# A hybrid attention block on one core: dense steps dealt out anew at the start of the attention, and GpSimd's low parts cut into four

## The chip, the core and the metric

The kernel runs on one core of one Trainium2 chip. TensorE multiplies matrices, VectorE and ScalarE work on tiles and read the products out of PSUM, GpSimd does a few elementwise operations and issues some of the DMAs, SyncE issues most of the others. The engines run side by side, each through its own instructions in a fixed order, and wait for each other by semaphores. The metric is the device time in microseconds (us) of one execution; less is better.

## The reference

One layer on 512 tokens of width 1024, in float32. `proj` is split into queries, keys and values of two attentions and into two gates; both attentions are gated, merged and followed by a feed-forward network and a gated embedding.

```python
proj = rms_norm(x, g_mix[i]) @ w_in[i]
(q_n, kc_n, vc_n, ks_n, vs_n, kw_n, vw_n, gate_n,
 q_m, k_m, v_m, gate_a, gate_b) = jnp.split(proj, IN_CUTS, axis=-1)
y_nsa = nsa_mixer(q_n, kc_n, vc_n, ks_n, vs_n, kw_n, vw_n, gate_n, pos_pad, ...)[:, :s]
y_moba = moba_mixer(q_m, k_m, v_m, pos_pad, ...)[:, :s]
merged = (jax.nn.sigmoid(gate_a[:, :s]) * (y_nsa @ w_up_nsa[i])
          + jax.nn.sigmoid(gate_b[:, :s]) * (y_moba @ w_up_moba[i]))
x = x + merged @ w_out[i]
gate, up = jnp.split(rms_norm(x, g_ffn[i]) @ w_ffn_in[i], 2, axis=-1)
x = x + (jax.nn.silu(gate) * up) @ w_ffn_out[i]
ple_gate = jax.nn.sigmoid(rms_norm(x, g_ple[i]) @ w_ple_gate[i])
x = x + ple_gate * (p[i] @ w_ple_proj[i])
```

With 512 tokens the attentions come down to causal softmax attention: 8 heads of MoBA with one set of keys, and 8 heads of NSA with two sets (selected and window) and 32 compressed keys besides.

## The kernel before

**Number format.** A float32 operand is split into a high part (`wh`, rounded to float32r by ScalarE, L128) and a low part (`wl`, the rest, by subtraction, L133 or L135). A product is three matmuls: high by high, high by low, low by high (`tmm`, L466 to L472). `Weights` keeps a list of weight units of 128x1024. SyncE's DMAs bring them into `wr` (three buffers); `get` splits units ahead of use (`depth` 2, in the attention 3) into `wh` and `wl` (four buffers each). Low parts are made by VectorE. Only for units of the kinds "ga" and "um", once `between` is set, GpSimd makes them (L131 to L133), in its order behind a one-column copy called "seen" (L977) of the last job's normalized probabilities. `between` is set for the first time after the attention's third step. GpSimd also issues the DMAs that add blocks of feed-forward weights in memory for a later stage (`add`, L278 and L281), each behind a "seen".

**The attention.** `attention(jobs)` (from L880) is a generator that yields after each step. It runs 24 jobs, 8 of MoBA and 16 of NSA; there are 192 steps. A job has four score tiles `sb`, for query tiles 3, 2, 0 and 1, of 512, 384, 128 and 256 columns; each is two matmuls (L893 with the key's high part, L894 with the low one). The tiles of 384 and 128 columns lie in one PSUM bank, and two banks take turns. VectorE masks a tile and finds its extreme (L896, into `p` and `am`), ScalarE takes the exponential (L898), and `normalize` (L903 to L913) scales by one over the sum, three tiles on VectorE and the one of 512 columns on ScalarE (L911). Then `turn` transposes the ten blocks of `p` (L921, tile `pt`), which are split into `pw` and `phl` (L930 ScalarE, L931 VectorE), and `apply` multiplies them by the values (L940 to L945, tile `pv`). `finish_head` (L867 to L876) adds the halves of a head's result and splits pairs of heads into YM or YN: `yt` on ScalarE, `yf` on VectorE, the high part on ScalarE, the low part on VectorE. `KN` (L548, L549) are keys of NSA that a side chain still turns meanwhile.

**The dense steps.** `fill` is a chain of the gate products (`gates`, tiles `ga`, 16 weight units) and MoBA's projection (`up`, tiles `umo`, 4 units). A step is one `tmm` of 3 x 512 columns; 8 steps make a unit, 160 the whole chain. Its purpose is work for TensorE that needs nothing of the softmax. The order in which steps are issued is written by hand at L1040 to L1045. `weave` deals out a share of a dense step per attention step: 0.95 for the first 80, 0.65 after (FILL_RATE, L35), and a quarter of a step of the side chain. Dense steps left over stand behind the attention. Behind all this comes NSA's projection (tiles `uno`), whose last quarter needs the last pair of heads.

**The order on the engines.** The framework puts the instructions of all engines into order by its own estimate of when each can run, starting from the order of issue; `issue_after` adds constraints, among them that a dense step stands behind the scores or transposes issued before it (`anchors`). So a moved step changes the order on TensorE, VectorE and ScalarE at other places, too.

Of the kernel before, what the change touches and what calls it, by code (L numbers as in the profile page):

```python
# [10 lines left out]
F32 = mybir.dt.float32  # L11
# [3 lines left out]
OP = mybir.AluOpType  # L15
# [16 lines left out]
WARM = 9  # L32
BIG_BUFS = 34
AHEAD = 7
FILL_RATE = (0.95, 0.65, 80)  # L35
BEFORE_UM = 3
BEGUN = 2
SCALE = "vvva"
# [23 lines left out]
class Weights:  # L62
# [42 lines left out]
    def parts(self):  # L105
        i = self.n_split
        self.load(i + 1)
        self.n_split += 1
        key, src, n, tag = self.units[i]
        if isinstance(src, str):  # L110
            t, q = (self.kept[x] for x in src.split("+"))
            with self.tc.issue_after(self.low):
                self.nc.vector.tensor_add(t[:, :n], t[:, :n], q[:, :n])
        else:
            t = self.raw.pop(i)
        if key[0] == "fo" and not isinstance(src, str):
            self.kept[key[3]] = t
        if isinstance(src, tuple) and None in src:
            k = 512 * src.index(None)
            with self.tc.issue_after(self.low):  # L120
                self.nc.vector.tensor_add(t[:, k:k + 512], self.last[:, :512], self.last[:, 512:])  # L121
        self.last = t
        h = self.pool.tile([128, 1024], F32R, name=f"wh{i}", tag="wh", bufs=4)
        l = self.pool.tile([128, 1024], F32R, name=f"wl{i}", tag="wl", bufs=4)
        self.done[i] = (h, l)
        for a, b in self.pieces(i, n):
            for c, d in self.halves(i, n) if i else [(a, b)]:
                self.begun = self.nc.scalar.activation(h[:, c:d], t[:, c:d], AF.Copy).ins  # L128
            if i == a == 0:
                yield  # L130
            if self.between is not None and key[0] in ("ga", "um"):  # L131
                with self.tc.issue_after(self.between):
                    self.low = self.nc.gpsimd.tensor_tensor(l[:, a:b], t[:, a:b], h[:, a:b].bitcast(F32), op=OP.subtract).ins  # L133
            else:
                self.low = self.nc.vector.tensor_sub(l[:, a:b], t[:, a:b], h[:, a:b].bitcast(F32)).ins  # L135
            yield
# [17 lines left out]
def run(gen):  # L154
    for _ in gen:
        pass


def weave(main, side, ratio=1.0, later=None, turn=0):

    acc, alive = 0.0, True
    for n, _ in enumerate(main):
        acc += ratio if later is None or n < turn else later
        while acc >= 1.0 and alive:
            acc -= 1.0
            try:
                next(side)
            except StopIteration:
                alive = False
        yield  # L170
    if alive:
        yield from side
# [8 lines left out]
def chain(*gens):  # L181
    for g in gens:
        yield from g
# [12 lines left out]
def steps(gen, n):  # L196
    for _ in range(n):
        next(gen, None)
# [18 lines left out]
def hybrid_kernel(ctx: ExitStack, tc: tile.TileContext, a, out):  # L217
# [333 lines left out]
    def turned(parts, tag, dst, gain):  # L551


        b = bank("tb", tag)
        for t, x in enumerate(parts):
            T.transpose(b[:, tts(t)], x, ident)
        for i in range(2):
            half = slice(64 * i, 64 * i + 64)
            last = split_turned((b[half], half), dst[:, i], gain)
        return last  # L560
# [118 lines left out]
    def gates(i0, i1, tag="a"):  # L679
        for i in range(i0, i1):  # L680
            o = bank("ga", tag)
            yield from ttile(("ga", i), o)
            z = GT[i]
            V.tensor_tensor(z, o, rb0, op=OP.mult)
            A.activation(z, z, AF.Tanh)
# [324 lines left out]
    def up(nm, Y, done):  # L1010
        for i in range(4):
            wh, wl = W.get((nm, i))
            os = []
            for j in range(2):
                o = bank(nm + "o", "a")
                os.append(o)
                for kt in range(4):
                    tmm(o, wh, wl, j * 4 + kt, Y[0][kt], Y[1][kt], kt == 0, kt == 3)
                    yield
                done(2 * i + j, o)  # L1020
# [9 lines left out]
    att = attention(jobs)  # L1030
# [9 lines left out]
    fill = chain(gates(8, 16), gates(0, BEFORE_UM), up("um", YM, up_moba_done), gates(BEFORE_UM, 8))  # L1040
    W.depth = 3
    steps(fill, 4)
    steps(att, 1)
    steps(fill, 4)
    run(weave(weave(att, fill, *FILL_RATE), side, 0.25))  # L1045

# [170 lines left out]
    class Blocks:  # L1217
# [14 lines left out]
        def split(self, j, *parts):  # L1232
            for src, names in parts:
                n = len(names) * CH
                nm = f"{self.name}{j}{names[0]}"
                if n == 1024:
                    h, l = flat(t4(nm + "h")), flat(t4(nm + "l"))
                elif n == 512:
                    r = t4(nm)
                    h, l = r[:, 0], r[:, 1]  # L1240
                else:
                    if j % 2 == 0:
                        self.third = t4(nm)
                    h, l = (self.third[:, j % 2, half(k)] for k in range(2))
                A.activation(h, src, AF.Copy)
                V.tensor_sub(l, src, h.bitcast(F32))  # L1246
                for k, x in enumerate(names):
                    self.at[j, x] = h[:, half(k)], l[:, half(k)]
# [278 lines left out]
```

## Time and profile before

| | |
|---|---|
| median of three runs | 815.98 us (815.6 to 816.95) |
| the profiled execution's own time | 815.51 us |
| its span, from the first to the last instruction | 813.8 us |
| attention with dense steps, from its first scores to its last product | 147.2 to 354.7 us of the span |
| GpSimd's 16 low parts | 160.2 to 324.0 us of the span, 2.39 to 2.69 us each |
| granted TensorE clock | 1.00 |

The profile is one execution. PE is TensorE's matmuls, PEld its weight loads, DVE VectorE, ACT ScalarE, POOL GpSimd. A timeline row has start, duration, engine, line, operation, output and inputs; in brackets stands the idle time of the engine ahead of it and what ended that. Ends of matmuls are modelled, so they overlap; the distance between starts tells the pace. Line numbers are those of the kernel before; in the changed kernel they are 2 higher from L133 on, and 4 higher from L1044 on.

### The profile page before, as it was taken

How to read it: one execution, taken by the hardware profiler on the slowest of the kernel's cores; microseconds unless marked ns; L12 is line 12 of the kernel's file. 1: busy time of each engine (PE TensorE's matmuls, PEld its weight loads, DVE VectorE, ACT ScalarE, POOL GpSimd, SP SyncE). 2: the span in 40 equal slices, each digit the busy share in tenths (PEclk: the TensorE clock that was granted, in tenths of full speed). 3: DMA queues.
4: the chain of work that ended last, by engine and by line, in shares of the span. 5: the costliest groups of instructions: out<-in, count | busy, mean ns of one | idle time of the engine just before them, and what ended most of it. 6: DMA issues, size and time to landing. Idle time of an engine off the chain costs nothing.

```text
span 813.8 us, 13180 instructions
## 1 busy us (share of the span) xinstructions
PE 807.0 (99%) x4821; PEld 717.5 (88%) x4821; DVE 628.0 (77%) x1165; ACT 490.0 (60%) x941; POOL 177.7 (22%) x210
## 2 busy tenths in 40 slices
PE   9999999999999999999999999999999999999997
PEld 7889898788888888888888999988999989998886
DVE  6889777887777867849467888887888887889744
ACT  6456555867777777734366666644666644665631
POOL 2826245333333413116010011000111000010000
PEclk9999999999999999999999999999999999999999
DMA  9434659598877758645424244444344343461612
GB/s 339 160 121 125 216 137 281 168 235 231 222 240 153 222 144 211 168 126 176 182 89 149 78 130 131 143 145 139 114 146 133 129 155 117 131 233 66 195 38 91
DMA packets 45361, 130.43 MB, mean 160 GB/s; under 512 B 5232, under 2 KB 5616, under 8 KB 41328
## 3 DMA queue, kind: packets, MB, share of 16 engines
q1 hardware_dynamic: 39376, 92.87, 34.9%
q0 software_dynamic: 4416, 32.51, 16.1%
q10 hardware_dynamic: 1504, 4.21, 1.6%
q8 instruction: 38, 0.62, 0.3%
q14 instruction: 27, 0.22, 0.1%
HBM read 122.22 MB, written 36.70 MB: 195 GB/s over the span
## 4 chain that ended last, share of the span: by engine, by line
PE 98%; DVE 1%; DMA 0%; ACT 0%; issue 0%; SPq 0%
PE sa L472 5%; PE sa L471 5%; PE sa L470 5%; PE ga L470 4%; PE ga L472 4%; PE ga L471 4%; PE nt L1115 3%; PE nt L1117 3%; PE nt L1116 3%; PE pt L921 3%; PE sv L1381 2%; PE sv L1384 2%; PE sv L1383 2%; PE sc L472 2%; PE sc L471 2%; PE sc L470 2%
## 5 line engine op out<-in xcount | busy, mean ns | idle before, releaser
L128 ACT ACTIVATE wh<-wr 128x512 fp32r<-128x512 f32 (+2 forms) x263 | 204.4, 800 | 179.9 <-PE sc L471 29.5
L135 DVE TENSOR_TENSOR wl<-wr,wh 128x1024 fp32r<-128x1024 f32 (+2 forms) x187 | 215.5, 1162 | 69.6 <-ACT wh L128 68.2
L896 DVE CUSTOM_DVE_ANT_0 p<-sb,big_mask 128x512 f32<-128x512 f32 (+1 forms) x96 | 45.6, 486 | 13.2 <-PE sb L894 12.5
L470 PE MATMUL ga<-xh,wh 128*128 128x512 f32 x128 | 53.0, 414 | 0.0
L472 PE MATMUL ga<-xh,wl 128*128 128x512 f32 x128 | 50.2, 393 | 0.0
L471 PE MATMUL ga<-xl,wh 128*128 128x512 f32 x128 | 50.1, 391 | 0.0
L1299 POOL TENSOR_TENSOR hg<-zg,u 128x256 f32<-128x256 f32 x10 | 10.4, 1038 | 156.7 <-ACT zg L1298 156.7
L1299 POOL TENSOR_TENSOR hf<-zg,u 128x256 f32<-128x256 f32 x10 | 15.9, 1588 | 128.3 <-DVE h L1246 110.9
L133 POOL TENSOR_TENSOR wl<-wr,wh 128x1024 fp32r<-128x1024 f32 x16 | 40.7, 2542 | 0.1
L931 DVE TENSOR_TENSOR pw<-pt,pw 128x512 fp32r<-128x512 f32 x48 | 32.5, 685 | 7.7 <-ACT pw L930 7.6
L921 PE MATMUL pt<-ident,p 128*128 128x128 f32 x240 | 36.6, 273 | 0.0
L921 PEld LDWEIGHTS pt<-ident,p 128*128 128x128 f32 x240 | 29.0, 140 | 4.7 <-issue 0.2
L977 POOL COPY seen<-p 128x1 f32<-128x1 f32 x24 | 4.4, 183 | 125.7 <-DVE p L913 118.8
L930 ACT ACTIVATE pw<-pt 128x512 fp32r<-128x512 f32 x48 | 27.6, 591 | 5.1 <-PE pt L921 4.4
L472 PEld LDWEIGHTS ga<-xh,wl 128*128 128x128 f32 x128 | 24.0, 188 | 5.4
L121 DVE TENSOR_TENSOR wr<-wr 128x512 f32<-128x512 f32 x40 | 27.4, 686 | 0.0
L471 PEld LDWEIGHTS ga<-xl,wh 128*128 128x128 f32 x128 | 24.2, 189 | 3.4
L470 PEld LDWEIGHTS ga<-xh,wh 128*128 128x128 f32 x128 | 24.2, 189 | 3.4
L1115 PE MATMUL nt<-wh,x3h 128*128 128x512 f32 (+1 forms) x72 | 26.2, 370 | 0.0
L1116 PE MATMUL nt<-wl,x3h 128*128 128x512 f32 (+1 forms) x72 | 26.1, 367 | 0.0
L1117 PE MATMUL nt<-wh,ML 128*128 128x512 f32 x64 | 24.9, 389 | 0.0
L1115 PE MATMUL nt<-wh,MH 128*128 128x512 f32 x64 | 24.9, 389 | 0.0
(953 smaller groups left out, 2792.3 us busy)
## 6 DMA issues: line engine op xcount, KB each, us to landing
fi7s<-fi POOLq DMA_DIRECT2D x16, 1280.0 KB, 9.4
wr<-fi SPq DMA_DIRECT2D x60, 256.0 KB, 2.7
wr<-fi7s SPq DMA_DIRECT2D x40, 256.0 KB, 2.9
wr<-ga SPq DMA_DIRECT2D x16, 512.0 KB, 7.2
fos<-fo POOLq DMA_DIRECT2D x8, 1024.0 KB, 7.0
wr<-fo SPq DMA_DIRECT2D x15, 512.0 KB, 3.9
wr<-fos SPq DMA_DIRECT2D x10, 512.0 KB, 3.6
wr<-wo SPq DMA_DIRECT2D x8, 512.0 KB, 3.6
```

The lines of the kernel that those rows point to most:

```text
L128: self.begun = self.nc.scalar.activation(h[:, c:d], t[:, c:d], AF.Copy).ins
L133: self.low = self.nc.gpsimd.tensor_tensor(l[:, a:b], t[:, a:b], h[:, a:b].bitcast(F32), op=OP.subtract).ins
L135: self.low = self.nc.vector.tensor_sub(l[:, a:b], t[:, a:b], h[:, a:b].bitcast(F32)).ins
L470: T.matmul(o, wh[:, sl], h, start=start, stop=False, skip_group_check=skip)
L471: T.matmul(o, wh[:, sl], l, start=False, stop=False, skip_group_check=skip)
L472: return T.matmul(o, wl[:, sl], h, start=False, stop=stop, skip_group_check=skip).ins
L896: V.tensor_tensor_reduce(out=p, in0=o, in1=big_mask[:, 512 - n:512], op0=OP.add, op1=OP.min, scale=1.0, scalar=3.0e38, accum_out=st["m"][: ...
L921: last = T.transpose(b[:, off:off + 128], st["p"][:, P_OFF[qt] + kb * 128:P_OFF[qt] + kb * 128 + 128], ident)
L931: V.tensor_sub(pl, b[:, :off], ph.bitcast(F32))
L1115: T.matmul(o[:, cols], h[kt][:, tts(tt)], w1, start=kt == 0, stop=False)
L1116: T.matmul(o[:, cols], h[kt][:, tts(tt)], w2, start=False, stop=False)
L1117: T.matmul(o[:, cols], l[kt][:, tts(tt)], w1, start=False, stop=kt == KT - 1)
```

## The change

```diff
@@ -32,7 +32,7 @@
-FILL_RATE = (0.95, 0.65, 80)
+FILL_RATE = (0.95, 0.65, 72)
@@ -130,7 +130,9 @@
             if self.between is not None and key[0] in ("ga", "um"):
                 with self.tc.issue_after(self.between):
-                    self.low = self.nc.gpsimd.tensor_tensor(l[:, a:b], t[:, a:b], h[:, a:b].bitcast(F32), op=OP.subtract).ins
+                    for c in range(a, b, 256):
+                        x = slice(c, c + 256)
+                        self.low = self.nc.gpsimd.tensor_tensor(l[:, x], t[:, x], h[:, x].bitcast(F32), op=OP.subtract).ins
             else:
@@ -1040,7 +1042,9 @@
     W.depth = 3
     steps(fill, 4)
-    steps(att, 1)
+    for _ in range(5):
+        steps(att, 1)
+        steps(fill, 2)
     steps(fill, 4)
     run(weave(weave(att, fill, *FILL_RATE), side, 0.25))
```

Two dense steps are issued behind each of the first five attention steps, where before four stood behind the first and the weave went on from there. The weave's higher rate lasts 72 attention steps instead of 80. A low part that GpSimd makes is four instructions of 256 columns instead of one of 1024. Which units GpSimd takes stays the same, 16 in all; so do TensorE's instructions in number and kind, and SyncE's order.

On TensorE, at the second job of the attention (`sb` are scores, `ga` a dense step, numbers tell buffers apart), this stood before:

```order
L893 MATMUL sb<-KM_1012,QM_598 128x512
L894 MATMUL sb<-k2M_1400,QM_598 128x512
L470 MATMUL ga<-xh_116,wh_1663 128x512
L471 MATMUL ga<-xl_119,wh_1663 128x512
L472 MATMUL ga<-xh_116,wl_1664 128x512
L893 MATMUL sb<-KM_1012,QM_598 128x384
L894 MATMUL sb<-k2M_1400,QM_598 128x384
L893 MATMUL sb<-KM_1012,QM_598 128x256
L894 MATMUL sb<-k2M_1400,QM_598 128x256
L893 MATMUL sb<-KM_1012,QM_598 128x128
L894 MATMUL sb<-k2M_1400,QM_598 128x128
```

At the same job, from the second dense step behind its 512 columns on, it now reads:

```order
L472 MATMUL ga<-xh_125,wh_1663 128x512
L473 MATMUL ga<-xl_126,wh_1663 128x512
L474 MATMUL ga<-xh_125,wl_1664 128x512
L895 MATMUL sb<-KM_1012,QM_598 128x384
L896 MATMUL sb<-k2M_1400,QM_598 128x384
L923 MATMUL pt<-ident,p 128x128 x10
L895 MATMUL sb<-KM_1012,QM_598 128x256
L896 MATMUL sb<-k2M_1400,QM_598 128x256
L895 MATMUL sb<-KM_1012,QM_598 128x128
L896 MATMUL sb<-k2M_1400,QM_598 128x128
```

The second job's tiles no longer follow each other: two dense steps stand ahead of the 384 columns, and all ten transposes of the first job ahead of the 256 and the 128.

On VectorE, in the same place, the second job's tiles (`am__1744`) stood between a product of KN and the first job's normalization (`as__1687`):

```order
L896 ISA p,am__1686<-sb,big_mask 128x128
L896 ISA am__1686 128x1
L896 ISA p,am__1744<-sb,big_mask 128x512
L896 ISA am__1744 128x1
L549 SCALAR_TENSOR_TENSOR KN_509<-tb,kg,KN_509 64x512
L896 ISA p,am__1744<-sb,big_mask 128x384
L896 ISA am__1744 128x1
L903 TENSOR_SCALAR as__1687<-as__1687 128x4
```

Now it has these rows, with the second job's tiles named `am__1747`:

```order
L898 ISA p,am__1686<-sb,big_mask 128x128
L898 ISA am__1686 128x1
L905 TENSOR_SCALAR as__1687<-as__1687 128x4
L908 RECIPROCAL as__1687<-as__1687 128x4
L915 TENSOR_SCALAR p<-p,as__1687 128x128
L915 TENSOR_SCALAR p<-p,as__1687 128x256
L915 TENSOR_SCALAR p<-p,as__1687 128x384
L686 TENSOR_TENSOR GT_1725<-ga,rb 128x512
L898 ISA p,am__1747<-sb,big_mask 128x512
L898 ISA am__1747 128x1
L898 ISA p,am__1747<-sb,big_mask 128x384
L898 ISA am__1747 128x1
```

The first job is normalized before the second job's first tile, and KN comes later.

On TensorE, at the end of the attention, the last head's product (`pv`, from `phl`) was followed by the last matmul of a dense step and by 27 of NSA's projection (`uno`) ahead of the first one that needs the last heads; its first rows:

```order
L940 MATMUL pv<-phl,VN_511 128x256
L943 MATMUL pv<-PC_2751,VC 128x512
L944 MATMUL pv<-PC_2751,VC 128x512
L945 MATMUL pv<-phl,VN_511 128x256
L472 MATMUL ga<-xh_137,wl_3700 128x512
L470 MATMUL uno<-YNh_3008,wh_3833 128x512
L471 MATMUL uno<-YNl_3010,wh_3833 128x512
L472 MATMUL uno<-YNh_3008,wl_3834 128x512
```

Now no dense step is left there, and 18 of the projection's matmuls follow before the last heads are needed:

```order
L942 MATMUL pv<-phl,VN_511 128x256
L945 MATMUL pv<-PC_2849,VC 128x512
L946 MATMUL pv<-PC_2849,VC 128x512
L947 MATMUL pv<-phl,VN_511 128x256
L472 MATMUL uno<-YNh_3064,wh_3954 128x512
L473 MATMUL uno<-YNl_3066,wh_3954 128x512
L474 MATMUL uno<-YNh_3064,wl_3955 128x512
```

The first weight of the projection (`wh_3833` before, `wh_3830` now) is now used up ahead of the last product, and the second (`wh_3954`) begins right behind it.

## The prediction

> **What bounds the kernel now.** I read the page's engine totals first, then its row of the clock, then the chain that ended last.
>
> ```profile
> span 813.8 us, 13180 instructions
> PE 807.0 (99%) x4821; PEld 717.5 (88%) x4821; DVE 628.0 (77%) x1165; ACT 490.0 (60%) x941; POOL 177.7 (22%) x210
> PEclk9999999999999999999999999999999999999999
> PE 98%; DVE 1%; DMA 0%; ACT 0%; issue 0%; SPq 0%
> ```
>
> TensorE is busy for 807.0 of 813.8 us at full clock, and 98% of the chain is its own work. Only 6.8 us are idle, so an edit that adds or removes no matmul can bring at most what TensorE waits, and can lose any amount. The change touches the attention stage alone. So the next views are the busy times by stretch (columns: stretch, its length, busy time and count of each engine, clock, DMA) and TensorE's waits.
>
> ```profile
> 150.00:160.00 10.00, 9.13 (x50) 7.62 (x49) 8.39 (x31) 9.36 (x25) 1.24 (x4) 1.00 0.17 49
> 160.00:200.00 40.00, 39.99 (x229) 34.50 (x229) 32.93 (x88) 28.89 (x65) 13.67 (x13) 1.00 0.89 243
> ...
> PE warm L355 <- DVE half_neg L389: 1.2, 1, 1.2
> PE sb L893 <- DVE am__1744 L896: 0.9, 1, 0.9
> PE qm L460 <- ACT wh L128: 0.3, 1, 0.3
> PE sv L1381 <- DVE X L1360: 0.2, 1, 0.2
> ```
>
> Of the four waits only the second lies in the attention stage, and it accounts for the 0.87 us missing from 150 to 160 us; the 40 us behind it are full. The timeline shows how it comes about.
>
> ```profile
> 153.74 0.74 DVE L549 SCALAR_TENSOR_TENSOR KN<-tb,kg,KN 64x512 fp32r<-64x512 f32 x1
> 153.85 0.30 PE L893 MATMUL sb<-KM,QM 128*128 128x256 f32 x1
> ...
> 153.98 0.28 PE L894 MATMUL sb<-k2M,QM 128*128 128x256 f32 x1
> 154.51 0.56 DVE L896 CUSTOM_DVE_ANT_0 p<-sb,big_mask 128x384 f32<-128x384 f32 x1
> ...
> 155.14 0.33 PE L893 MATMUL sb<-KM,QM 128*128 128x128 f32 x1 [0.87 <-DVE am__1744 L896]
> ```
>
> The 128-column scores share a PSUM bank with the 384-column ones, and are written only after VectorE has read those. VectorE is late: it first finishes a KN product, 0.74 us long, and reads the 384 columns until 155.07. From 153.98 to 155.14 are 1.16 us between two starts that are 0.13 apart for the pair before: **1.03 us lost**.
>
> A second place is visible only on the weight loads, where VectorE is held up beside GpSimd.
>
> ```profile
> 179.04 2.69 POOL L133 TENSOR_TENSOR wl<-wr,wh 128x1024 fp32r<-128x1024 f32 x1
> 179.71 2.58 DVE L876 TENSOR_TENSOR YMl<-yf,YMh 128x512 fp32r<-128x512 f32 x1 [0.24 <-ACT YMh L875]
> 182.21 0.68 DVE L931 TENSOR_TENSOR pw<-pt,pw 128x512 fp32r<-128x512 f32 x1
> 182.95 0.19 PEld L945 LDWEIGHTS pv<-pw,VM 128*128 128x128 f32 x1 [0.25 <-DVE pw L931]
> ```
>
> L876 takes 2.58 us here and 0.69 in its last instance (quoted with the attention's end below); it ends 0.56 us after GpSimd's 2.69 us are over. Its 1.89 us of delay push the low part pw back, and TensorE's weight load for L945 waits 0.25 us.
>
> **The change part by part: the dense steps.** No instruction of TensorE is added or removed; 160 dense steps and 192 attention steps are dealt out anew. Before, seven dense steps lay behind the first five attention steps (four behind the first, then 0.95 each); now ten do, two behind each, and four more follow at once. The rows for the new timing are these.
>
> ```profile
> 147.22 0.39 PE L893 MATMUL sb<-KM,QM 128*128 128x512 f32 x1
> ...
> 147.68 0.39 PE L470 MATMUL ga<-xh,wh 128*128 128x512 f32 x1
> ...
> 148.36 0.39 PE L470 MATMUL ga<-xh,wh 128*128 128x512 f32 x1
> ...
> 148.82 0.68 DVE L896 CUSTOM_DVE_ANT_0 p<-sb,big_mask 128x512 f32<-128x512 f32 x1
> ...
> 150.37 1.06 ACT L128 ACTIVATE wh<-wr 128x1024 fp32r<-128x1024 f32 x1
> ...
> 152.46 0.49 ACT L898 ACTIVATE p<-p,am__1686 128x256 f32<-128x256 f32 x1
> ...
> 153.52 0.39 ACT L898 ACTIVATE p<-p,am__1686 128x128 f32<-128x128 f32 x1
> ...
> 156.55 0.71 ACT L911 ACTIVATE p<-p,as__1687 128x512 f32<-128x512 f32 x1
> ...
> 156.62 0.08 DVE L896 DVE_READ_ACCUMULATOR2_ANT am__1744<- 128x1 f32 x1
> 156.62 0.88 DVE L913 TENSOR_SCALAR p<-p,as__1687 128x128 f32<-128x128 f32 x3
> ```
>
> A dense step is 0.68 us (147.68 to 148.36) for 1536 columns; other products are worked out by their columns at this rate, twice each, once per half of the key. All before 147.22 stands as it was, so TensorE now runs: job 0's first scores (512 columns, 0.45), two steps, the 384 and 256 columns (0.57), two steps, the 128 columns (0.11), two steps, job 1's 512 (0.45), two steps, its 384 (0.34). It reaches the ten transposes of job 0 at 147.22 + 0.45 + 4 x 1.36 + 0.57 + 0.11 + 0.45 + 0.34 = 154.6. VectorE starts at 148.82 as before and has read the 384 columns by about 150.1; the 128-column scores come at 151.0, so **the old wait has 0.9 us of cover**. KN has left this place: its transposes now stand ten rows behind the first products. This removes 1.03 us. A wait would be next at the transposes, which need job 0 normalized: the four exponentials end near 152.1 (the 128 columns are read at 151.6, then 0.39 and its accumulator), VectorE's two short steps and 0.88 us of scaling end near 153.4, and ScalarE's split of a weight (1.06) with its scaling (0.71) near 153.9. That is 0.7 us ahead of 154.6. Job 1's 128 columns, after the transposes, come near 155.9, with VectorE done with its 384 near 155.4. Neither waits by these numbers.
>
> Behind this the rates are the old ones, 0.95 and later 0.65 dense steps per attention step; the lower one sets in after 72 steps instead of 80. Of 160 dense steps, 18 + 68.4 + 74.75 = 161 are now dealt out before the attention ends, against 8 + 76 + 72.15 = 156: none is left behind it. I bound what this creates or removes in small waits by the weight loads' row for L945 (0.25, quoted): from none to three of them, 0 to 0.8 us, and take 0.1, near none, since the full 160 to 200 us has the same rates.
>
> **The change part by part: GpSimd.** Sixteen low parts become four pieces each.
>
> ```profile
> L133 POOL TENSOR_TENSOR wl<-wr,wh 128x1024 fp32r<-128x1024 f32 x16 | 40.7, 2542 | 0.1
> L1299 POOL TENSOR_TENSOR hg<-zg,u 128x256 f32<-128x256 f32 x10 | 10.4, 1038 | 156.7 <-ACT zg L1298 156.7
> ...
> 302.74 2.40 POOL L133 TENSOR_TENSOR wl<-wr,wh 128x1024 fp32r<-128x1024 f32 x1
> ...
> 322.01 0.40 PE L472 MATMUL ga<-xh,wl 128*128 128x512 f32 x1
> ```
>
> A piece was not run before: a quarter of 2.54 us is 0.64, and the nearest row of its size is 1.04. So a unit takes 2.5 to 4.2 us; I take 1.04, the row with the same shape: 16 x (4.15 - 2.54) = 26 us more on GpSimd. It lies beside TensorE's work: the smallest distance between a low part's end and its first reader, weight unit 17, is 322.01 - 305.14 = 16.9 us, ten times the growth. If that cover were gone, each unit would cost TensorE its 1.6 us. Behind the pieces on GpSimd wait only the next "seen" copies and the DMAs that add weight blocks for a later stage. What the pieces bring is that VectorE can be held for one piece instead of 2.69 us: L876's delay falls from 1.89 to at most 1.04 us, and the 0.25 us at L945 goes. Since two transposes would have taken 0.22 of the 0.39 us from 182.56 (their start) to 182.95, 0.17 to 0.25 are regained; I take 0.2.
>
> [...]
>
> **The sum:** 1.03 + 0.2 - 0.1 = 1.1 us less. The profiled execution took 815.51 us (its span of 813.8 and 1.7 around it), which becomes 814.4; it lies 0.47 below the median of the three runs, 815.98. Against that median the forecast is **814.9 us**, 0.13% less.
>
> **The rivals.** *More is regained*: all waits of the weight loads go, with L945 a second time (another 0.25) and the first term at 1.16: 1.16 + 0.25 + 0.25 = 1.66, 814.3 us. For it speaks that VectorE gets slack in both places, against it that a new order brings small waits of its own. *The wait only moves* to the ten transposes in a row, where all of job 0 must be normalized: 0.7 us of cover is less than one weight split of 1.06. If one more split, or a KN product, stands in front, about 1 us comes back: 815.9. *The attention's end* turns it slower.
>
> ```profile
> 354.46 0.28 PE L945 MATMUL pv<-phl,VN 128*128 128x256 f32 x1
> ...
> 355.21 0.59 ACT L869 ACTIVATE yt<-pv 64x512 f32<-64x512 f32 x1
> 356.85 0.68 DVE L873 TENSOR_TENSOR yf<-pv,yt 64x512 f32<-64x512 f32 x1
> 357.57 0.63 ACT L875 ACTIVATE YNh<-yf 128x512 fp32r<-128x512 f32 x1 [1.22 <-DVE yf L873]
> 358.24 0.69 DVE L876 TENSOR_TENSOR YNl<-yf,YNh 128x512 fp32r<-128x512 f32 x1 [0.70 <-ACT YNh L875]
> ...
> 360.94 1.07 PE L470 MATMUL uno<-YNh,wh 128*128 128x512 f32 x4
> ```
>
> The last head's result is ready 3.74 us after its last product starts (358.20), and 28 matmuls cover 6.5 us. Now only 18 stand there: 0.11 + 18 x 0.227 = 4.2 us. Cover remains as long as product and copies take under 4.2 us; alone they need 0.28 + 0.59 + 0.68 + 0.63 = 2.2, the rest was queueing behind a weight's split. If one more split stands in front (1.06 us on ScalarE by the row above, and as an estimate as much on VectorE), they take 5.9, TensorE waits 1.7 us, and the time is 815.98 - 1.1 + 1.7 = 816.6.
>
> **How the numbers follow.** The forecast 0.62 (814.4 to 815.3), more regained 0.16, moved 0.14, the end 0.08. The range of 813.9 to 816.5 leaves out half of the last and the tails of the others. About 0.2% (1.6 us) is what a measurement of this kernel can tell from no change. Faster by more than that: most of "more regained" and the forecast's edge, 0.18. Slower: the end case with a second wait, 0.06. Within: 0.76.
>
> **What would show it.** Right: no wait at L893 (then L895) from 150 to 160 us, TensorE full there, no VectorE instruction stretched past 1.8 us beside the low parts, GpSimd's busy time up by 7 to 26 us. Wrong: a wait of TensorE at the ten transposes (L923), at the last uno matmuls, or a first use of a low part that waits for GpSimd.

## The result: 0.56% slower

The changed kernel took **821.09 us** in the median of six runs (819.52 to 821.77), the kernel before 816.25 beside it (815.60 to 817.27, six runs): a ratio of 1.0056, 95% interval 1.0045 to 1.0067. The forecast was 814.9, its range 813.9 to 816.5. In the experiments below, one execution of one kernel (dense steps only, L907 as four) took 1619.9 us, twice the others, and is left out of that kernel's ratio.

The lines of the page of after that answer to those of before, and the groups of GpSimd's low parts and of the transposes (columns: out<-in, count | busy us, mean ns | idle us before, and what ended it):

```profile
span 817.8 us, 13226 instructions
PE 808.2 (99%) x4821; PEld 717.3 (88%) x4821; DVE 635.5 (78%) x1165; ACT 489.9 (60%) x941; POOL 183.6 (22%) x258
...
PEclk9999999999999999999999999999999999999999
...
L135 POOL TENSOR_TENSOR wl<-wr,wh 128x256 fp32r<-128x256 f32 x64 | 47.1, 869 | 0.1
...
L923 PE MATMUL pt<-ident,p 128*128 128x128 f32 x240 | 36.5, 273 | 2.1 <-DVE pw L933 2.0
```

VectorE has as many instructions as before and 7.5 us more busy time: 635.5 against 628.0. Something stretches its steps. Four rows of the attention are far above their like (0.69 us, and 0.16 for L907):

```profile
187.81 4.06 DVE L824 TENSOR_TENSOR CD<-CD,cu__2133 128x512 f32<-128x512 f32 x1
...
204.49 3.17 DVE L878 TENSOR_TENSOR YMl<-yf,YMh 128x512 fp32r<-128x512 f32 x1
```

The other two, L812 and L907, are shown further on (2.97 and 2.44 us). Together the four are 10.4 us over; in before it was two rows, L876 with 2.58 us and L810 with 1.23, 2.4 us over. The first two cost TensorE nothing here; it is full around them (5.00 of 5 us from 187 us on, 4.00 of 4 from 204 on). The transposes now wait 2.0 us for the low part `pw`. The same stretches of time in after and, below, in before, with the busy time of TensorE first:

```profile
150.00:160.00 10.00, 9.99 (x54) 8.40 (x53) 7.11 (x28) 8.21 (x22) 3.56 (x6) 1.00 0.48 173
...
200.00:230.00 30.00, 28.76 (x165) 24.58 (x163) 27.26 (x66) 20.89 (x48) 9.26 (x16) 1.00 0.67 185
...
270.00:300.00 30.00, 27.98 (x159) 24.20 (x158) 24.56 (x71) 21.13 (x51) 11.25 (x20) 1.00 0.64 170
300.00:360.00 60.00, 59.71 (x336) 51.28 (x335) 44.27 (x128) 43.15 (x101) 12.63 (x23) 1.00 0.64 170
```

```profile
200.00:230.00 30.00, 30.00 (x170) 26.21 (x169) 22.05 (x67) 21.38 (x49) 12.00 (x11) 1.00 0.88 221
...
270.00:300.00 30.00, 30.00 (x173) 26.14 (x172) 22.56 (x71) 22.21 (x54) 8.38 (x10) 1.00 0.66 176
300.00:360.00 60.00, 60.00 (x332) 51.64 (x331) 41.44 (x119) 39.85 (x92) 13.48 (x17) 1.00 0.65 172
```

The first stretch is full, as was forecast: 9.99 against 9.13 us. The others lost: 1.24, 2.02 and 0.29 us, in places that before were full. TensorE's three largest waits of after, in the attention, are these (total, times, longest, in us):

```profile
PE pt L923 <- DVE pw L933: 2.0, 1, 2.0
...
PE sb L895 <- DVE am__2445 L898: 0.9, 1, 0.9
PE sb L895 <- DVE am__2553 L898: 0.3, 1, 0.3
```

The largest, in the timelines of VectorE, GpSimd and TensorE (start, duration):

```profile
278.06 0.68 DVE L898 CUSTOM_DVE_ANT_0 p<-sb,big_mask 128x512 f32<-128x512 f32 x1
278.67 0.08 DVE L898 DVE_READ_ACCUMULATOR2_ANT am__3227<- 128x1 f32 x1
278.67 2.44 DVE L907 SCALAR_TENSOR_TENSOR as__3150<-as__3150,ginv 128x4 f32<-128x4 f32 x1
...
281.56 0.68 DVE L933 TENSOR_TENSOR pw<-pt,pw 128x512 fp32r<-128x512 f32 x1
```

```profile
278.27 2.80 POOL L135 TENSOR_TENSOR wl<-wr,wh 128x256 fp32r<-128x256 f32 x4
```

```profile
279.88 0.40 PE L942 MATMUL pv<-pw,VN 128*128 128x512 f32 x1
282.30 0.44 PE L923 MATMUL pt<-ident,p 128*128 128x128 f32 x2 [2.02 <-DVE pw L933]
```

L907 multiplies four sums per row by the gate. Its other fifteen instances take 0.16 to 0.17 us. This one takes 2.44 us and ends 0.04 us after the four pieces of a low part are over. The read of PSUM just ahead of it (L898), which reaches into the first piece, kept its 0.68 us. Behind L907 in VectorE's order stands the low part `pw`, and the next transposes, which write into that bank, waited 2.02 us for it. The wait at 221 us has the same shape: L812, the compressed scores minus their extreme, takes 2.97 us beside four pieces, and the reads of the score tiles stand behind it.

```profile
216.91 2.97 DVE L812 TENSOR_TENSOR CD<-CD,cm__2542 128x512 f32<-128x512 f32 x1
...
220.62 0.56 DVE L898 CUSTOM_DVE_ANT_0 p<-sb,big_mask 128x384 f32<-128x384 f32 x1
```

So the theory: **VectorE is held beside GpSimd's low parts, four pieces hold it as one, and the new order put held steps ahead of what TensorE needs next.** Rivals: the pieces cost by themselves; the new order costs by itself, whatever GpSimd does. Left open by this profile: it is the fastest of the six runs, at a granted clock of 1.000; the other five had 0.997 or 0.998 and took 820.58 to 821.77.

### The profile page after: what moved, and what is told of

The parts are those of the page before. It is cut to its first block, busy times and chain, and to the rows that moved or that the text cites. A ratio compares the mean times of both kernels' runs of the same rounds, so it can differ in the third digit from the quotient of the medians.

```text
span 817.8 us, 13226 instructions
## 1 busy us (share of the span) xinstructions
PE 808.2 (99%) x4821; PEld 717.3 (88%) x4821; DVE 635.5 (78%) x1165; ACT 489.9 (60%) x941; POOL 183.6 (22%) x258
## 4 chain that ended last, share of the span: by engine, by line
PE 86%; DVE 7%; DMA 3%; ACT 1%; POOL 1%; issue 1%; SPq 0%; DVEq 0%; ACTq 0%
PE sa L474 5%; PE sa L473 5%; PE sa L472 5%; PE nt L1121 3%; PE nt L1120 3%; PE nt L1119 3%; PE pt L923 3%; PE ga L472 3%; PE ga L474 2%; PE ga L473 2%; PE sv L1385 2%; PE sv L1387 2%; PE sv L1388 2%; PE sc L474 2%; PE sc L473 2%; PE sc L472 2%
## 5 line engine op out<-in xcount | busy, mean ns | idle before, releaser
L898 DVE CUSTOM_DVE_ANT_0 p<-sb,big_mask 128x512 f32<-128x512 f32 (+2 forms) x96 | 45.1, 481 | 13.3 <-PE sb L896 12.9
L135 POOL TENSOR_TENSOR wl<-wr,wh 128x256 fp32r<-128x256 f32 x64 | 47.1, 869 | 0.1
L1303 POOL TENSOR_TENSOR hg<-zg,u 128x256 f32<-128x256 f32 x10 | 10.4, 1036 | 159.3 <-ACT zg L1302 159.3
L1303 POOL TENSOR_TENSOR hf<-zg,u 128x256 f32<-128x256 f32 x10 | 13.6, 1361 | 128.0 <-DVE h L1250 110.9
L923 PE MATMUL pt<-ident,p 128*128 128x128 f32 x240 | 36.5, 273 | 2.1 <-DVE pw L933 2.0
L923 PEld LDWEIGHTS pt<-ident,p 128*128 128x128 f32 x240 | 28.9, 140 | 6.7 <-DVE pw L933 2.3
```

The lines of the kernel that those rows point to most:

```text
L135: self.low = self.nc.gpsimd.tensor_tensor(l[:, x], t[:, x], h[:, x].bitcast(F32), op=OP.subtract).ins
L898: V.tensor_tensor_reduce(out=p, in0=o, in1=big_mask[:, 512 - n:512], op0=OP.add, op1=OP.min, scale=1.0, scalar=3.0e38, accum_out=st["m"][: ...
L923: last = T.transpose(b[:, off:off + 128], st["p"][:, P_OFF[qt] + kb * 128:P_OFF[qt] + kb * 128 + 128], ident)
```

## The experiments

Each ratio is to runs of the kernel before on the same chip (its medians 816.07 to 816.30 us), with a 95% interval; 0.001 is 0.8 us. "CD steps" are the two wide steps on the compressed scores, L812 and L824.

| kernel | us, median | ratio |
|---|---|---|
| before, pieces only | 817.78 | 1.0016 (1.0007 to 1.0024) |
| dense steps only, whole low parts | 817.43 | 1.0015 (1.0006 to 1.0023) |
| changed, two pieces of 512 | 817.69 | 1.0019 (1.0010 to 1.0028) |
| dense steps only, rate change after 80 | 818.56 | 1.0029 (1.0017 to 1.0041) |
| changed, L907 as four small steps | 817.52 | 1.0018 (1.0009 to 1.0027) |
| dense steps only, L907 as four | 815.47 | 0.9992 (0.9983 to 1.0001) |
| the same once more | 815.91 | 1.0000 (0.9991 to 1.0009) |
| before, pieces and memsets | 816.81 | 1.0005 (0.9996 to 1.0014) |
| changed, with memsets | 817.68 | 1.0019 (1.0011 to 1.0028) |
| changed, once more | 820.78 | 1.0050 (1.0037 to 1.0064) |
| changed, L907 as four, CD steps on GpSimd | 816.08 | 1.0001 (0.9992 to 1.0010) |
| dense steps only, the same two edits | 815.72 | 0.9995 (0.9986 to 1.0004) |
| changed, all low parts on VectorE | 817.01 | 1.0010 (1.0001 to 1.0019) |
| before, L907's like (L905) as four | 816.78 | 1.0006 (0.9997 to 1.0014) |

The whole time also varies with what lies ahead of the attention: the first scores start between 147.2 and 149.4 us in the 16 profiles, though TensorE's 791 matmuls before them are the same in the same order. So a second measure is given where it helps, the **stage**: from the start of the first scores to that of the first product behind NSA's projection (tile `nt`), 1248 matmuls in every kernel. It took 227.33 us in before's profile (147.22 to 374.55) and 230.62 in after's (147.96 to 378.58). It is one profile each; two profiles of one kernel, the dense steps with L905 as four, gave 226.81 and 226.89.

### One part of the change at a time

The pieces alone:

```diff
-  self.low = self.nc.gpsimd.tensor_tensor(l[:, a:b], t[:, a:b], h[:, a:b].bitcast(F32), op=OP.subtract).ins
+  for c in range(a, b, 256):
+      x = slice(c, c + 256)
+      self.low = self.nc.gpsimd.tensor_tensor(l[:, x], t[:, x], h[:, x].bitcast(F32), op=OP.subtract).ins
```

> The kernel before with GpSimd's low parts in four pieces of 256 columns and nothing else; every other engine keeps its order. Theory 'order' (the new order brings VectorE's short steps beside GpSimd's low parts at places where TensorE soon needs them; four pieces on end hold VectorE about as long as one whole, 2.8 to 3.1 us against 2.5): nearly nothing, 816.0 to 817.0, and the delay of L876 at 180 us stays near 2.5 us or grows, since VectorE is not served between two pieces. Theory 'pieces' (cutting the low parts is what costs, more and longer holds of VectorE): most of the 4.8 us, 819.5 to 821. Prediction's step: the delay at L876 falls to 1.04 us or less and 0.2 us are won, 816.0.

1.3 us slower (0.6 to 2.0): between the two theories, and against the prediction's step. VectorE, GpSimd and TensorE's weight loads at the place that the prediction had chosen:

```profile
180.41 3.00 DVE L878 TENSOR_TENSOR YMl<-yf,YMh 128x512 fp32r<-128x512 f32 x1 [0.24 <-ACT YMh L877]
183.33 0.68 DVE L933 TENSOR_TENSOR pw<-pt,pw 128x512 fp32r<-128x512 f32 x1
```

```profile
179.74 3.11 POOL L135 TENSOR_TENSOR wl<-wr,wh 128x256 fp32r<-128x256 f32 x4
```

```profile
184.07 0.19 PEld L947 LDWEIGHTS pv<-pw,VM 128*128 128x128 f32 x1 [1.09 <-DVE pw L933]
```

The pieces follow on each other, and the step ends 0.56 us after the last of them is over, as it did after the whole low part: 3.00 us instead of 2.58, with 3.11 us for four pieces and 2.69 for one whole low part. The weight load's wait grew from 0.25 to 1.09 us. The order on TensorE, VectorE and ScalarE is that of before, so this is the pieces' doing. The stage is 0.9 us longer (228.25).

The dense steps alone, then the changed kernel with pieces of 512, which has the same order on TensorE, VectorE and ScalarE:

```diff
-  for c in range(a, b, 256):
-      x = slice(c, c + 256)
-      self.low = self.nc.gpsimd.tensor_tensor(l[:, x], t[:, x], h[:, x].bitcast(F32), op=OP.subtract).ins
+  self.low = self.nc.gpsimd.tensor_tensor(l[:, a:b], t[:, a:b], h[:, a:b].bitcast(F32), op=OP.subtract).ins
...
-  for c in range(a, b, 256):
-      x = slice(c, c + 256)
+  for c in range(a, b, 512):
+      x = slice(c, c + 512)
```

> The changed kernel with GpSimd's low parts whole again (1024 columns): the dense steps alone. The order of TensorE differs from the changed kernel's in some 90 rows of 4810, since the scheduler reckons with GpSimd's times. Theory 'order': the loss is there without the pieces, 819 to 822, with a wait of TensorE at transposes or at 128-column scores between 160 and 300 us behind a VectorE step held by a whole low part. Theory 'pieces': the dense steps alone win the 1.0 us at 154 us, 815.0 to 815.6. In between, 816 to 819, the two parts meet: which VectorE steps stand beside the low parts is a matter of each order.

> The changed kernel with the low parts in two pieces of 512 columns; its order on TensorE, VectorE and ScalarE is that of the kernel with whole low parts, not that of the four pieces. Theory 'order': the same time as with whole low parts within 0.7 us, since pieces on end hold VectorE as one. Theory 'pieces': between whole and four pieces, 817 to 819. If VectorE is served between two pieces, it lies below the one with whole low parts.

1.2 us slower (0.5 to 1.9) and 1.6 us (0.8 to 2.3), the same within their intervals. Two pieces hold L907 as one whole does (2.17 us, to the end of the second at 278.65; TensorE then waits 1.76 us for `pw`). The 1.0 us at 154 us is won in both, and lost again at one place, here of the kernel with whole low parts:

```profile
276.95 2.06 DVE L905 SCALAR_TENSOR_TENSOR as__3114<-as__3114,ginv 128x4 f32<-128x4 f32 x1
...
279.46 0.69 DVE L931 TENSOR_TENSOR pw<-pt,pw 128x512 fp32r<-128x512 f32 x1
```

```profile
276.57 2.41 POOL L133 TENSOR_TENSOR wl<-wr,wh 128x1024 fp32r<-128x1024 f32 x1
```

```profile
280.20 0.44 PE L921 MATMUL pt<-ident,p 128*128 128x128 f32 x2 [1.65 <-DVE pw L931]
```

The small step is held by a whole low part (276.57 to 278.98) as it is by four pieces. So each part of the change loses by itself, some 1.3 us. Together they lose more than the sum: in the profiles at full clock the stage is 0.9 us longer with the pieces, 1.1 with the dense steps (228.40) and 3.3 with both. For the framework, which reckons with GpSimd's times, makes yet another order out of both, and in that one L812 is held as well, ahead of the reads of a score tile.

Another order of the same work, the dense steps alone with the old rate change:

```diff
-FILL_RATE = (0.95, 0.65, 72)
+FILL_RATE = (0.95, 0.65, 80)
```

> Whole low parts, two dense steps behind each of the first five attention steps, but the lower rate sets in after 80 steps as before: another order of the same work. Theory 'order' (chance meetings of VectorE steps with low parts): anything from 814.8 to 821, with the difference to the kernel with 72 steps explained by single waits of TensorE of 0.3 to 2 us that follow a VectorE step stretched past 2 us. Rival (the dense steps at the start cost by themselves, wherever the lower rate sets in): the same time as with 72 steps within 0.5 us.

2.4 us slower (1.4 to 3.3). L905 is held again, another instance (2.13 us at 294.10), and TensorE waits 2.36 us at 298.22. In all three orders with the dense steps some instance of this small step is held ahead of a `pw`; in before's order none is (0.15 to 0.17 us for all sixteen).

### What is held, and whether a gap lets VectorE in

L907 rewritten, in the changed kernel and in the dense steps alone:

```diff
-  V.scalar_tensor_tensor(s, s, 1e-30, job["gate"], op0=OP.max, op1=OP.mult)
+  for qt in range(QT):
+      V.tensor_scalar(s[:, qt:qt + 1], s[:, qt:qt + 1], 1e-30, job["gate"][:, qt:qt + 1], op0=OP.max, op1=OP.mult)
```

> The changed kernel with the step L907 (the sums of the exponentials times ginv, 128x4, both operands in SBUF) written as four VectorE steps on 128x1 with ginv as the scalar operand; TensorE's order differs in 13 rows of 4810. Theory 'two operands': beside a GpSimd low part VectorE is held only in an instruction that reads two SBUF tensors (L878, L812, L824, L907 and L137 were stretched; those that read PSUM or one tensor kept their times). So nothing is held at 278.7 us, the 2.0 us wait at L923 goes, and 821.1 becomes 819.1 (818.3 to 819.6); if TensorE's lower clock (0.998) in five of six runs came from that wait, 817.5. Rival 'any step': whatever stands there on VectorE is held to the end of the four pieces: 820.5 to 821.5, with a wait at L923 of some 2 us.

> The dense steps alone (whole low parts) with the same rewriting of that step into four 128x1 steps with a scalar operand. Theory 'two operands': the 1.6 us wait at the transposes at 280 us goes: 817.4 becomes 815.8 (815.2 to 816.3), below the kernel before by at most 0.1%. Rival 'any step': 817.0 to 817.8, the wait stays.

821 fell to 817.5, and 817.4 to 815.5. In both, the wait at 280 us is gone; in the second nothing is held for 2 us any more; the one stretched row is that of three scalings, 1.46 us at 278.72 instead of 0.88. VectorE and GpSimd in the changed kernel with that edit:

```profile
279.83 0.21 DVE L908 TENSOR_SCALAR as__3168<-as__3168,ginv 128x1 f32<-128x1 f32 x1
280.07 0.18 DVE L909 RECIPROCAL as__3168<-as__3168 128x4 f32<-128x4 f32 x1
280.24 0.69 DVE L934 TENSOR_TENSOR pw<-pt,pw 128x512 fp32r<-128x512 f32 x1
280.84 1.86 DVE L916 TENSOR_SCALAR p<-p,as__3168 128x128 f32<-128x128 f32 x3
```

```profile
279.20 2.83 POOL L135 TENSOR_TENSOR wl<-wr,wh 128x256 fp32r<-128x256 f32 x4
```

The small steps pass, the low part `pw` (one operand in PSUM) passes and frees TensorE, and only the scaling behind it is held: 1.86 us for three instructions that took 0.88 in before. So "any step is held" is out, but so is "only a step that reads two SBUF tensors": L916 reads one, and a 128x1 scalar. What decides which steps are held, no run here shows.

Pieces with a GpSimd memset between them, which reads nothing, in the kernel before and in the changed one:

```diff
...
+  if c + 256 < b:
+      with self.tc.issue_after(self.low):
+          gap = self.pool.tile([128, 1], F32, name=f"gap{i}_{c}", tag="gap", bufs=1)
+          last = self.nc.gpsimd.memset(gap, 0.0).ins
```

> The kernel before with pieces of 256, and between two pieces a GpSimd memset of 128x1, which reads nothing; the order of TensorE, VectorE and ScalarE is unchanged. Theory 'pieces on end hold as one': the pieces follow each other without a gap, so VectorE is not served between them; behind a memset it is: L878 at 180 us takes 0.9 to 1.8 us instead of 3.0, the wait of 0.85 us at L947 goes, 817.8 becomes 816.3 to 817.0. Rival 'the hold does not end between instructions of GpSimd, whatever they are': L878 takes 3.0 to 3.4 us, 817.5 to 818.3.

> The changed kernel with a memset of 128x1 between two pieces; TensorE's order differs in 40 rows of 4810. Theory 'pieces on end hold as one': L907 falls from 2.44 us to 1.2 or less, L812 from 2.97 to 1.8 or less, so that the waits at L923 (2.0) and L895 (0.9) shrink by 1.2 and 0.9: 821.1 becomes 819.0 (818.0 to 819.8). Rival 'the hold does not end between instructions': 821 to 822.

VectorE and GpSimd in the first of them:

```profile
182.07 2.81 DVE L883 TENSOR_TENSOR YMl<-yf,YMh 128x512 fp32r<-128x512 f32 x1 [0.24 <-ACT YMh L882]
```

```profile
181.14 1.03 POOL L136 TENSOR_TENSOR wl<-wr,wh 128x256 fp32r<-128x256 f32 x1
181.82 0.38 POOL L140 MEMSET gap<- 128x1 f32 x1
181.88 1.00 POOL L136 TENSOR_TENSOR wl<-wr,wh 128x256 fp32r<-128x256 f32 x1
...
183.35 0.97 POOL L136 TENSOR_TENSOR wl<-wr,wh 128x256 fp32r<-128x256 f32 x1
```

By these records the memset lies across the end of one piece and the start of the next (181.82 to 182.20, while the one piece ends at 182.17 and the other starts at 181.88): GpSimd's instructions overlap, and there is no gap. The step ends 0.56 us after the last piece (184.32), as without memsets. My theory of what would let VectorE in fell here, although the time, 816.8, lies in the range that it gave: the step starts 0.93 us behind the first piece instead of 0.67, so that the weight load waits 0.76 us instead of 1.09, the stage is 0.6 us longer than before's instead of 0.9, and whether this kernel is slower than before at all is not shown (0.3 us faster to 1.1 slower). In the changed kernel it is the same: the small step (there L912) is held for 2.20 us, a YMl step that begins in the middle of a group ends 0.56 us after the group's end, and TensorE waits 1.79 us at 280 us. That its time fell all the same, by 3 us where I had expected 2, has other reasons: the wait at 221 us is not there in its slightly different order, and the clock was 0.999 or more in all runs. What a true gap between pieces would do was not tried.

All low parts on VectorE ("the pair" is VectorE and GpSimd):

```diff
-  if self.between is not None and key[0] in ("ga", "um"):
+  if False:
```

> The changed kernel with all low parts on VectorE, none on GpSimd: no instruction of VectorE can be held, but VectorE gets 16 more steps of 1.22 us, 19.5 us, in the attention. Theory 'the pair': the waits behind L907, L812 and L878 go; if VectorE has room for 19.5 us, 815 to 817. Rival 'GpSimd's help is worth more than its holds': VectorE, busy for some 80 of 100 us there, is late elsewhere: 818 to 824, with waits of TensorE for VectorE spread over the attention and none of them behind a stretched step.

0.8 us slower than before (0.1 to 1.6), and 3.8 us below the changed kernel's 820.8: no step is held for long in the attention (one row of three scalings takes 1.36 us instead of 0.88, beside another step of GpSimd's, L817), and TensorE's largest wait there is 0.6 us. So VectorE has room for most of the 19.5 us. Without the holds GpSimd's help may still be worth something: the dense steps with whole low parts on GpSimd and L905 as four steps took 815.5 and 815.9, in another order.

### The clock

> The changed kernel once more, on the chip of the next three, since five of its six runs had a granted clock of 0.998 and its profiled run, with 1.000, was the fastest. Theory 'the stall lowers the clock': again most runs at 0.998 and 820.5 to 821.8. Rival 'the clock of those runs was a matter of that chip or hour': clocks of 0.999 to 1.000 as in the experiments so far, and 818.8 to 819.8, about 1.9 us above the kernel with the four 128x1 steps (817.5).

4.1 us slower (3.0 to 5.2), with clocks of 1.000, 0.999, 0.998, 0.998 and 0.997: the lower clock comes with this kernel, not with one chip. The profiled run is one at 0.998. Busy times by microsecond, TensorE first, the granted clock the third figure from the right:

```profile
280.00:281.00 1.00, 0.00 (x0) 0.00 (x0) 0.97 (x2) 0.07 (x1) 0.80 (x2) 1.00 0.95 393
281.00:282.00 1.00, 0.00 (x0) 0.00 (x0) 0.96 (x4) 0.72 (x1) 0.00 (x0) 1.00 0.94 324
282.00:283.00 1.00, 0.98 (x5) 0.94 (x6) 1.00 (x3) 0.38 (x1) 0.18 (x1) 0.87 0.74 233
283.00:284.00 1.00, 1.00 (x4) 0.71 (x4) 1.00 (x6) 0.34 (x1) 0.70 (x2) 0.50 0.67 270
284.00:285.00 1.00, 1.00 (x4) 0.81 (x3) 0.31 (x1) 0.86 (x4) 1.00 (x3) 0.50 0.27 33
285.00:286.00 1.00, 1.00 (x6) 0.80 (x5) 0.00 (x0) 0.00 (x0) 1.00 (x3) 0.50 0.93 139
286.00:287.00 1.00, 1.00 (x8) 0.87 (x7) 0.00 (x0) 0.00 (x0) 0.94 (x2) 0.92 0.83 172
```

Some 0.7 us after the matmuls have gone on, behind a wait of 2.04 us, the clock is halved for 3.4 us (0.26 us of the third stretch, 3 whole ones, 0.16 of the last): 0.13 + 3 x 0.50 + 0.08 = 1.7 us lost, on top of the wait itself. That is the distance between after's profiled run and its other five. By the mean clock of a run (1.7 of 819 us make it 0.998) the halving came in 8 of 11 runs of this kernel, in 1 of 7 of the kernel with a wait of 2.36 us (820.59 us at 0.997), in none of 11 with a wait of 1.79 us, and in none of 11 once L907 was four steps. The length of the wait alone does not decide it; what else does stays open.

### What was left

The two wide steps of the compressed scores on GpSimd as well, on top of L907's edit:

```diff
-  V.tensor_tensor(d3, d3, m.unsqueeze(2).to_broadcast([128, 16, NCMP]), op=OP.subtract)
+  G.tensor_tensor(d3, d3, m.unsqueeze(2).to_broadcast([128, 16, NCMP]), op=OP.subtract)
...
-  V.tensor_tensor(d3, d3, s.unsqueeze(2).to_broadcast([128, 16, NCMP]), op=OP.mult)
+  G.tensor_tensor(d3, d3, s.unsqueeze(2).to_broadcast([128, 16, NCMP]), op=OP.mult)
```

> The changed kernel with the four 128x1 steps, and with the two wide steps of the compressed scores that read two SBUF tensors (L812 CD minus cm, L824 CD times cu, 128x512) on GpSimd instead of VectorE. Theory 'the held step's queue': L812, held to 2.97 us at 217 us, keeps the score reads behind it back, and TensorE's waits of 0.9 and 0.3 us at 222 and 228 us come from that; with them gone 817.5 becomes 816.2 (815.8 to 816.8). Rival 'TensorE waits there for the order alone': the waits of 0.9 and 0.3 stay, 817.3 to 817.8.

816.1 us, no difference to before: the waits at 222 and 228 us are gone, as the theory of the held step had it, and with them all of the loss. Steps are still held (L819 for 2.90 us at 186 us, L878 for 2.34 at 204 us), but TensorE needs nothing soon that stands behind them: a hold costs only where it does. From 821 the steps down are L907 with its clock (about 3.4) and the wide steps (1.4). To the forecast of 814.9 there remains 1.2 us. The control (L905 as four steps in the kernel before) and two kernels with the dense steps alone ask where that is, one a repetition, one with both edits:

> The kernel before with the four 128x1 steps instead of L905's one, as a control: L905 was not held there, so the rewriting by itself should bring nothing; it moves 285 rows of TensorE's order. Then the dense steps' own worth is the difference to the same rewriting with dense steps (815.5). Theory 'the prediction's first term holds': 816.0 to 816.6 here, 0.5 to 1.1 us above that kernel, with the wait of 0.87 us at the 128-column scores at 155 us still there. Rival 'the rewriting itself wins the time': 815.0 to 815.6 here.

> The dense steps alone with the four 128x1 steps, once more: the first 11 runs gave 815.5 and a ratio to before of 0.9992 with an interval that reaches 1.0001. Theory (the first term, 1.0 us, is kept once nothing is held): 815.2 to 815.8, ratio 0.999. Rival (it was the spread of one set of runs): 816.0 to 816.6.

> The same with L810's and L822's wide steps of the compressed scores on GpSimd. In the dense steps alone they were not held, so moving them takes nothing away, only gives VectorE 2.8 us less to do: theory 'only a hold on the way to TensorE costs': 815.2 to 815.9, like the kernel without the move. Rival 'VectorE's load is what TensorE still waits for (0.3 to 0.5 us each at 150, 308 and 335 us)': 814.4 to 815.0.

The control does not win by the rewriting: 0.5 us slower (0.2 faster to 1.1 slower). It is no pure control, for its order is another one as well, with two waits of its own at transposes (0.5 us in all); the wait at 155 us is still there. The dense steps without held steps gave 815.5 and then 815.9: no difference to before that holds. Less load on VectorE brings nothing clear either (815.7). The waits of the weight loads from 143 to 360 us show where the rest is, in the dense steps alone with L905 as four steps, and below it in before:

```profile
PEld sb L893 <- DVE am__3850 L896: 0.7, 2, 0.5
PEld pt L922 <- PE sb L894: 0.4, 1, 0.4
PEld sb L893 <- DVE am__1686 L896: 0.3, 1, 0.3
PEld sb L893 <- DVE am__3487 L896: 0.3, 1, 0.3
```

```profile
PEld sb L893 <- DVE am__1744 L896: 1.1, 1, 1.1
PEld pv L945 <- DVE pw L931: 0.5, 2, 0.2
PEld pt L921 <- issue: 0.2, 1, 0.2
```

1.7 us now, 1.8 before. The one wait at 155 us is gone, and five small ones stand in its place, at 151, 308 and 335 us, all but one behind a VectorE read of a score tile. Part of the gain is there all the same: the stage took 226.8 and 226.9 us in the two profiles of this kernel and 226.8 with both edits, against 227.3 in before's one profile, some 0.5 us less. That is half of the 0.9 us that the prediction had for the dense steps (1.03 less 0.1). In the whole time it is lost: no kernel here beats the one before by more than the measurement can tell.

## Why the prediction was wrong, point by point

- **What bounds the kernel: right, but read one way.** "An edit ... can bring at most what TensorE waits, and can lose any amount" stood in it; then only the gains were sized from the trace.
- **The first term, 1.03 us: right at its place, about half of it left over the stage.** No wait at the 128-column scores, TensorE busy 9.99 of 10 us. But "neither waits by these numbers" looked at other tiles, and job 0's 256-column scores wait: 0.3 us of the weight loads at 150 us, for a read of the tile before (am__1686).
- **"What the pieces bring is that VectorE can be held for one piece instead of 2.69 us": this step failed.** The four pieces run without a gap and hold VectorE as one, and longer: 2.80 to 3.11 us against 2.39 to 2.69. The 0.2 us to be gained became a loss, 0.8 us more at the very weight load that was to be freed. The prediction's sign of being right, "no VectorE instruction stretched past 1.8 us beside the low parts", was missed too: four were, up to 4.06 us. No run shows the 0.2 us of the sum: in the kernel with the pieces alone the wait at that weight load grew from 0.25 to 1.09 us. That VectorE gets in between two GpSimd instructions on end was my estimate, which no run shows. I also did not ask which VectorE steps are held and which are not.
- **"I bound what this creates ... from none to three of them, 0 to 0.8 us, and take 0.1": this step failed most.** The bound was taken from a case in which a held step had a lot of cover: L876 was late by 1.89 us, and TensorE felt 0.25 of it. Where little covers it, the price of a held step comes near its whole delay: L907 and L812 were each late by 2.28 us, and TensorE waited 2.0 us at L923 and 0.9 at L895; then came a halved clock of 1.7. The reason given for "near none", that 160 to 200 us was full, was one of the old order. The new order was compared with the old one in two places, and not at all for what stands on VectorE beside the sixteen low parts. The evidence was in the profile: sixteen low parts of 2.5 us each and L876 held beside one of them; what had to be asked was which steps can fall beside the others in the new order.
- **GpSimd's own time: right in kind.** A piece took 0.87 us in the mean (forecast 0.64 to 1.04), but they overlap, so the sixteen groups grew by 6.4 us, not 26, and GpSimd's busy time by 5.9. The 7 us set as the least growth does not follow from the prediction's own 2.5 to 4.2 us for a unit, which begin at no growth. No first use of a low part waited.
- **The rivals.** The wait did move, but not to job 0's ten transposes, which had their cover; it moved to two transposes 127 us later. The attention's end, the case for slower, did not come: no wait at `uno`. The rival that was missing is one mechanism: a VectorE step, however small, held ahead of a bank that TensorE needs.
- **The clock** was taken as given. It was full in the one profile that the sum was made against.

## What to carry to other kernels

When an edit deals out work anew, list, over the whole region and not only where the edit aims, what stands beside each long instruction that has held a step in the profile (here GpSimd's low parts, 2.58 us for L876 instead of 0.69); price a hold by its full length unless cover is shown. Cutting one long instruction into pieces on the same queue freed nothing here, with or without a memset between the pieces. A wait of TensorE of 2.04 us cost 3.7 us in one profile here, with 1.7 us lost at half clock behind it, so look at the granted clock of several runs, not of one profile.

## What the runs showed of the hardware

- A 128x4 step of 0.16 us took 2.06 to 2.45 us beside GpSimd's subtraction in five kernels; a 128x1 step with a scalar operand (0.21 us), a reciprocal (0.18) and steps with an operand in PSUM (0.68 and 0.69) kept their times at the same place.
- GpSimd's records overlap: a piece of 256 columns shows about 0.7 or 1.0 us, yet four are through in 2.80 to 3.11 us, and with a memset between them the step beside them still took 2.81 us, to 0.56 us after the last piece.
- A wait of TensorE of 2.04 us was followed by 3.4 us at a granted clock of 0.50 (1.7 us lost); behind a wait of 2.02 us in another run of the same program the clock stayed at 1.00.
